# A hybrid decoder layer on one core: own buffers for the raw weights of odd pairs, another order of the early pairs, and low parts moved between VectorE and DMA

## The chip, the cores and the metric

The kernel runs on one core of one Trainium2 chip. The metric is the device time of one execution in microseconds (us). Three runs of the kernel before took 1780.92, 1787.42 and 1790.28 us; the median is 1787.42.

## The reference, cut to what matters

One decoder layer over 1040 positions (16 meta tokens and 1024 inputs) with 1024 channels: a convolution branch and a sparse attention branch are gated, merged and added to the stream, and a gated FFN follows. The change lies in the FFN's up projection:

```python
D_MODEL, D_FF, FFN_CONV_WIDTH = 1024, 2816, 3
...
h = rms_norm(stream, ffn_norm_g[l])
up = causal_depthwise_conv(h @ ffn_up[l], ffn_dw_w[l], ffn_dw_b[l])
a, b_ = jnp.split(up, 2, axis=-1)
stream = stream + (jax.nn.silu(a) * b_) @ ffn_down[l]
```

All data are float32. `h @ ffn_up` multiplies 1024 positions by 1024 x 5632 weights.

## The kernel before, in words

**Products in three parts.** Every float32 operand of a product is split into a high part (a cast to fp32r) and a low part (the operand less its high part). A product is the sum of high x high, high x low and low x high, all in fp32r. A low part is made in one of two ways: by one subtraction on VectorE, or "by DMA", by which ScalarE writes the negated high part into the tile (line 1134 or 1037) and a DMA that accumulates, issued by POOL, adds the raw operand to it (line 1137 or 1038).

**Seven products in place of eight.** The up projection is cut into 22 pairs of 128 output channels (`NPAIR`; one column block of `a` and its partner of `b_`). With the reduction in two halves and the positions in two halves, a pair is a 2 x 2 block product, done with seven products (Strassen's scheme in Winograd's form). The blocks of weights are called A11, A12, A22, N2, S3, S1, S4 (`NAMES`, line 1071). A11, A12 and A22 are pieces of the raw weights; N2, S3, S1 and S4 are sums of pieces, made by four VectorE instructions in place in the two raw tiles `ra` and `rb` of the pair (lines 1121 to 1124). The blocks of rows are B11, B21 and B22 (pieces of the normalized stream `xs2`) and T1 to T4 (sums of pieces: `t12` holds T1 and T2, `t34` holds T3 and T4). `rows_first` makes B11 and B21; `rows_second` (line 1052) makes the others, k tile by k tile (four of them), with high parts `h12`, `h34`, low parts `l12`, `l34`, and both parts of B22 in `B22`.

**Early pairs.** Six pairs (`EARLY`) have their first two products, A11 x B11 and A12 x B21, done ahead (`up_first`), when only the first half of the positions is normalized; their sums wait in tiles `ua`. While TensorE does these twelve products, the second half is normalized and `rows_second` makes the sums. The main loop then does five products for each early pair and seven for each later one. A product is 24 matmuls: four k tiles, two chunks of columns, three parts.

**The order of blocks.** `bseq` (line 1072) lists the blocks of weights in the order of their use. `make_block` (line 1107) makes one: it loads the pair's raw tiles if they are not there (line 1084, on SP's queue), makes the four sums when it comes to N2, casts the high part into the ring tile (line 1132, ScalarE) and makes the low part (line 1134 and 1137, or 1139 on VectorE). The ring has five tiles (`RB`), so blocks are made up to five ahead of their use (`block`, line 1143). The raw tiles share two buffers of tag `wr`: one pair fills them both, and the next pair's loads wait until the last block of this one is made. Blocks A11, A12 and A22 get their low part by DMA, all others on VectorE.

**Tiles and queues.** `ft` gives a tile from 31 buffers, `ft2` one from 7, `tmp` one from 4; a new tile waits until an old one of its kind is read for the last time. A scheduler that works on estimated times puts the instructions of each engine in a fixed order; `urgent()` raises their priority in it. On the chip each engine serves its row in that order and waits by semaphores. SP issues the loads, POOL the accumulating DMAs and the stores of the gated rows (`dB`, `dT`), each in its own row. PSUM has four slots of two banks for these products (`slot`); VectorE's additions (line 1193) free them. After a pair's products, `up_rows` does the convolution of width 3 (line 1219, VectorE), SiLU and the gate.

Of the kernel before, what the change touches and what calls it, by code (L numbers as in the profile page):

```python
# [79 lines left out]
def body(ctx: ExitStack, tc: tile.TileContext, xT, vecs, w_idx, w_v, w_conv, w_k, w_q, w_gate,  # L80
# [970 lines left out]

    def rows_second():

        for k in range(KH):
            b11, b12, b21, b22 = (xs2[o + k][:, c] for o in (0, KH) for c in (c_lo, c_hi))
            t12, t34 = tmp(f"t12_{k}"), ft(f"t34_{k}")
            h12, l12, h34, l34 = (ft(f"{n}_{k}", F32R) for n in ("h12", "l12", "h34", "l34"))
            t = ft(f"B22_{k}", F32R)
            dve.tensor_tensor(t12[:, h0], b12, b11, op=ALU.subtract)
            dve.tensor_tensor(t12[:, h1], b22, t12[:, h0], op=ALU.subtract)  # L1060
            dve.tensor_tensor(t34[:, h1], b21, t12[:, h1], op=ALU.subtract)
            split_block(h34[:, h1], l34[:, h1], t34[:, h1], "T4", k)
            split_block(h12[:, h1], l12[:, h1], t12[:, h1], "T2", k)
            dve.tensor_tensor(t34[:, h0], b22, b12, op=ALU.subtract)
            split_block(h34[:, h0], l34[:, h0], t34[:, h0], "T3", k)
            split_block(h12[:, h0], l12[:, h0], t12[:, h0], "T1", k, True)
            split_block(t[:, h0], t[:, h1], b22, "B22", k, True)


    RB = 5  # L1070
    NAMES = ("A11", "A12", "A22", "N2", "S3", "S1", "S4")
    bseq = [(i, n) for i in range(EARLY) for n in ("A11", "A12")]
    for i in range(NPAIR):
        bseq += [(i, n) for n in NAMES if i >= EARLY or n not in ("A11", "A12")]
    bseq += [(k, "d" + n) for n in NAMES[:-1] for k in range(NG2)]
# [3 lines left out]
    w0, w1 = slice(0, WB), slice(WB, 2 * WB)  # L1079
    raws = {}  # L1080

    def raw_tile(name, src):
        t = base.tile([P, 2 * WB], F32, tag="wr", bufs=2, name=name)
        nc.sync.dma_start(t.rearrange("p (k n) -> p k n", k=src.shape[1]), src)
        return t

# [20 lines left out]
    def make_block():  # L1107
# [3 lines left out]
        if n[0] == "d":  # L1111
            raw = down_raw(i, n[1:])
        else:
            both = i >= EARLY or j >= 2 * EARLY
            if (i, 0) not in raws:
                raws[i, 0] = raw_tile(f"ra{i}", w_up[2 * i])
                if both:
                    raws[i, 1] = raw_tile(f"rb{i}", w_up[2 * i + 1])
            ra, rb = raws[i, 0], raws.get((i, 1))
            if n == "N2":  # L1120
                dve.tensor_tensor(ra[:, w0], ra[:, w0], rb[:, w0], op=ALU.subtract)
                dve.tensor_tensor(rb[:, w0], rb[:, w0], rb[:, w1], op=ALU.add)
                dve.tensor_tensor(rb[:, w1], ra[:, w0], rb[:, w1], op=ALU.subtract)  # L1123
                dve.tensor_tensor(ra[:, w1], ra[:, w1], rb[:, w1], op=ALU.add)
            raw = (ra if n in ("A11", "A12", "S3", "S4") else rb)[:, w0 if n in ("A11", "S3", "S1") else w1]
            if n == "S4":
                del raws[i, 0], raws[i, 1]
            elif n == "A12" and not both:
                del raws[i, 0]
        t = ring[j % RB]  # L1130
        with urgent():
            hi = act.copy(t[:, w0], raw)  # L1132
            if n in ("A11", "A12", "A22"):
                act.activation(t[:, w1], f(t)[:, w0], AF.Copy, scale=-1.0)  # L1134
                a = w_up[2 * i + (n == "A22")]
                kk = slice(0, KH) if n == "A11" else slice(KH, KT)
                pool.dma_start(t[:, w1].rearrange("p (k n) -> p k n", k=KH), a[:, kk], accum_op=ALU.add)  # L1137
            else:
                dve.tensor_tensor(t[:, w1], raw, f(t)[:, w0], op=ALU.subtract)
        if j < RB:  # L1140
# [129 lines left out]
    merge_half(1)  # L1270
    del zh, zl
    norm_half(1)
    for i in range(EARLY):
        early[i] = up_first(i, ft2(f"ua{i}"))
    rows_second()
    xs2.clear()
# [202 lines left out]
```

## Time and profile before

| | |
|---|---|
| median of 3 runs | 1787.42 us (1780.92 to 1790.28) |
| profiled execution | 1788.24 us, span 1786.5 us |
| TensorE busy | 1738.8 us (97% of the span), mean granted clock 0.985 |
| VectorE busy | 1279.8 us (72%) |
| ScalarE busy | 1074.4 us (60%) |
| POOL busy | 282.6 us (16%) |

The span is the time from the first to the last instruction in the profile; the execution's own time lies a little above it. Times in the rows below are in us from the span's start. The merge's last products end at 1086 us, the early products run to 1122.9, the main loop of the up projection to 1553, and the down projection fills the rest. TensorE is busy nearly always, so what matters is where it is not, and at which clock it runs.

### The profile page before, as it was taken

To read this page: it belongs to the slowest core of one execution; us is meant where nothing else is said; L and a number is where in the kernel's file an instruction comes from. 1 tells how busy PE (TensorE), PEld (TensorE's weight loads), DVE (VectorE), ACT (ScalarE), POOL (GpSimd) and SP (SyncE) were. 2 spreads that over 40 slices of the span, in tenths; PEclk is the share of its full clock that TensorE was granted. 3 is DMA by queue.
4 is the path that set the end of the run, shared out by engine and by line. 5 is a ranking of instruction groups with operands and counts; after the bars stand their busy time and mean duration, and the time that the engine had idled before them with its cause. 6 is when DMAs were issued, how large, how long until landed. Compare 5 with 4: busy or idle time off the path is not lost.

```text
span 1786.5 us, 30351 instructions
## 1 busy us (share of the span) xinstructions
PE 1738.8 (97%) x11836; PEld 1676.7 (94%) x11836; DVE 1279.8 (72%) x2107; ACT 1074.4 (60%) x1845; POOL 282.6 (16%) x368
## 2 busy tenths in 40 slices
PE   8999899999999999999999999989999999999997
PEld 8899799999999999899999999889999999988877
DVE  5695598996954493487853465799888888889765
ACT  6766678888998733488842245645455445544561
POOL 1110111111121112122100002212222222110030
PEclk8999999999999999999999999899999999999999
DMA  5653468776656488511246648545544554883372
GB/s 185 143 107 92 107 153 186 168 165 157 159 134 153 125 202 242 142 49 49 79 117 183 207 125 189 113 136 155 155 128 128 150 130 125 284 328 95 94 171 95
DMA packets 93472, 263.72 MB, mean 148 GB/s; under 512 B 10968, under 2 KB 19472, under 8 KB 93328
## 3 DMA queue, kind: packets, MB, share of 16 engines
q0 software_dynamic: 35872, 102.83, 28.3%
q1 hardware_dynamic: 57456, 158.95, 26.9%
q8 instruction: 93, 1.52, 0.3%
q14 instruction: 51, 0.42, 0.1%
HBM read 189.78 MB, written 47.53 MB: 133 GB/s over the span
## 4 chain that ended last, share of the span: by engine, by line
PE 71%; issue 14%; DVE 6%; DMA 5%; ACT 2%; POOL 1%; SPq 0%; POOLq 0%; DVEq 0%; ACTq 0%
PE PS L183 31%; PE PS L1158 21%; PE PS L1002 5%; PE PS L1287 3%; PE PS L914 3%; PE PS L858 3%; PE PS L892 2%; PE PS L460 1%; ACT junk L511 1%; DMA x<-dx 1%; DVE cum L566 1%; DMA rb<-w_up 0%; DMA co<-ct 0%; PE PS L307 0%; DMA ring<-w_up 0%
## 5 line engine op out<-in xcount | busy, mean ns | idle before, releaser
L1158 PE MATMUL PS<-h,ring 128*128 128x256 f32 (+1 forms) x1408 | 191.7, 285 | 11.4 <-DMA ring<-w_up 7.6
L511 ACT ACTIVATE junk<-sc,wn 128x1040 bf16<-128x1040 f32 (+6 forms) x217 | 182.3, 840 | 27.3 <-DVE wn L535 14.4
L183 PE MATMUL PS<-hh,wh 128*128 128x342 f32 (+2 forms) x1096 | 193.4, 327 | 5.2 <-ACT gt L721 1.7
L1158 PE MATMUL PS<-B,ring 128*128 128x256 f32 (+1 forms) x1584 | 195.9, 284 | 0.0
L183 PE MATMUL PS<-hh,wl 128*128 128x342 f32 (+2 forms) x1096 | 192.5, 327 | 3.5 <-DMA wl<-w_conv 3.5
L1158 PEld LDWEIGHTS PS<-B,ring 128*128 128x128 f32 x1584 | 193.6, 192 | 0.0
L1158 PEld LDWEIGHTS PS<-h,ring 128*128 128x128 f32 x1408 | 179.3, 192 | 13.3 <-issue 8.1
L183 PE MATMUL PS<-hl,wh 128*128 128x342 f32 (+2 forms) x1096 | 190.1, 324 | 0.9 <-DMA hl<-x 0.9
L183 PEld LDWEIGHTS PS<-hh,wh 128*128 128x128 f32 x1096 | 179.4, 190 | 9.8 <-ACT gt L721 2.5
L183 PEld LDWEIGHTS PS<-hh,wl 128*128 128x128 f32 x1096 | 180.6, 191 | 5.3 <-DMA wl<-w_conv 3.8
L183 PEld LDWEIGHTS PS<-hl,wh 128*128 128x128 f32 x1096 | 177.3, 188 | 3.3 <-DMA hl<-x 1.7
L127 ACT CAST wh<-wr 128x1024 fp32r<-128x1024 f32 x79 | 82.7, 1046 | 132.9 <-PE PS L183 70.8
L606 DVE SCALAR_TENSOR_TENSOR cb<-g,dwh,cb 128x1026 f32<-128x1026 f32 x105 | 134.4, 1282 | 35.4 <-DMA cb<-ct 35.3
L606 DVE SCALAR_TENSOR_TENSOR co<-g,dwh,co 128x1026 f32<-128x1026 f32 x113 | 144.2, 1281 | 7.6 <-DMA co<-ct 7.5
L1287 PE MATMUL PS<-hlT,ring 128*128 128x512 f32 x528 | 123.1, 394 | 1.1 <-ACT hlT L1242 1.1
L1287 PEld LDWEIGHTS PS<-hlT,ring 128*128 128x128 f32 x528 | 99.0, 188 | 24.6 <-ACT hlT L1242 1.5
L1137 POOL DMA_DIRECT2D ring<-w_up x66 | 58.0, 884 | 327.7 <-ACT ring L1134 207.5
L1132 ACT CAST ring<-ra 128x512 fp32r<-128x512 f32 x88 | 54.2, 617 | 80.8 <-PE PS L1158 62.3
L1158 PE MATMUL PS<-l,ring 128*128 128x258 f32 x704 | 101.7, 287 | 1.1 <-DVE l L1040 1.1
L1132 ACT CAST ring<-rb 128x512 fp32r<-128x512 f32 x66 | 40.9, 620 | 96.2 <-DVE rb L1123 40.4
L1158 PEld LDWEIGHTS PS<-l,ring 128*128 128x128 f32 x704 | 93.0, 194 | 1.4 <-DVE l L1040 1.4
L1193 DVE TENSOR_TENSOR ua<-ua,PS 128x514 f32<-128x514 f32 x66 | 45.2, 685 | 53.0 <-PE PS L1158 53.0
(480 smaller groups left out, 3650.3 us busy)
## 6 DMA issues: line engine op xcount, KB each, us to landing
ring<-w_up POOLq DMA_DIRECT2D x66, 256.0 KB, 4.4
ra<-w_up SPq DMA_DIRECT2D x28, 512.0 KB, 3.6
rb<-w_up SPq DMA_DIRECT2D x22, 512.0 KB, 3.8
dT<-dt POOLq DMA_DIRECT2D x44, 256.0 KB, 4.0
hlT<-dT SPq DMA_DIRECT2D x44, 256.0 KB, 2.7
dB<-us POOLq DMA_DIRECT2D x33, 256.0 KB, 3.8
dth<-gt SPq DMA_DIRECT2D x16, 513.0 KB, 7.7
gate<-dth SPq DMA_DIRECT2D x16, 513.0 KB, 4.7
```

The source lines that it names most:

```text
L127: e = act.copy(wh[:, :nk * P], raw[:, :nk * P])
L183: pe.matmul(ps[:, ci, :n], lhsT=ww[:, sl], rhs=rr[k][:, c0:c0 + n], start=(k == 0 and pi == 0), stop=(k == nk - 1 and pi == 2))
L511: act.activation(junk[:, :n], sc[j][:, PAD:PAD + n], AF.Sign, bias=bits.bitcast(F32)[:, slot[j]:slot[j] + 1], accum_out=cnt[:, slot[j]:slo ...
L606: dve.scalar_tensor_tensor(a, g[:, w:w + LQ], wt[w], a, op0=ALU.mult, op1=ALU.add)
L858: pe.matmul(lg[:, :nn], lhsT=qq[:, qc], rhs=kk[g][:, c0:c0 + nn], start=(pi == 0), stop=(pi == 2))
L914: pe.matmul(ov[:, q0:2 * P], lhsT=vv[g][:, vs], rhs=tt[kb // 4][:, rs_], start=False, stop=(kb == nkb - 1 and pi == 2))
L1002: pe.matmul(ps[:, b, p0:p0 + nn], lhsT=ww[:, k * P:(k + 1) * P], rhs=rr[k][:, c0 + r0:c0 + r0 + nn], start=(k == 0 and pi == 0), stop=(k = ...
L1132: hi = act.copy(t[:, w0], raw)
L1137: pool.dma_start(t[:, w1].rearrange("p (k n) -> p k n", k=KH), a[:, kk], accum_op=ALU.add)
L1158: pe.matmul(ps[:, b, p0:p0 + nn], lhsT=t[:, o + k * P:o + (k + 1) * P], rhs=B[rows][k][e][:, r0:r0 + nn], start=(pi == 0 and k == 0), stop ...
L1193: return dve.tensor_tensor(dst, a, ps, op=op)
L1287: pe.matmul(ps[:, :n], lhsT=w[:, o + m * P:o + (m + 1) * P], rhs=r[:, x * HS + c0:x * HS + c0 + n], start=(k == 0 and pi == 0), stop=(k == ...
```

## The change

Four things are changed, all in the making of the up projection's operands.

1. `raw_tile` takes a source of tiles. In the main loop the raw tiles of odd pairs (all but the last) come from `ft` (pair 1: `ft2`); even pairs keep the two `wr` buffers.
2. The early pairs' first products are done in reverse order, pair 5 first and pair 0 last, and pair 0 loads both its raw tiles then and keeps them for its later blocks.
3. `rows_second` is cut in two loops. The first, with raised priority, makes T1, T2 and T4 and T4's high part for all four k tiles. The second makes all the rest; T1's and B22's low parts are now made on VectorE.
4. The first six blocks get their low parts on VectorE, and S3, S1 and S4 of the six early pairs get theirs by DMA, from the raw tile that holds the sum.

```diff
@@ -1051,25 +1051,35 @@
 
     def rows_second():
 
-        for k in range(KH):
-            b11, b12, b21, b22 = (xs2[o + k][:, c] for o in (0, KH) for c in (c_lo, c_hi))
-            t12, t34 = tmp(f"t12_{k}"), ft(f"t34_{k}")
-            h12, l12, h34, l34 = (ft(f"{n}_{k}", F32R) for n in ("h12", "l12", "h34", "l34"))
+        ks = range(KH)
+        t12, t34, h34 = [], [], []
+        with urgent():
+            for k in ks:
+                b11, b12, b21, b22 = (xs2[o + k][:, c] for o in (0, KH) for c in (c_lo, c_hi))
+                t12.append(tmp(f"t12_{k}"))
+                t34.append(ft(f"t34_{k}"))
+                h34.append(ft(f"h34_{k}", F32R))
+                dve.tensor_tensor(t12[k][:, h0], b12, b11, op=ALU.subtract)
+                dve.tensor_tensor(t12[k][:, h1], b22, t12[k][:, h0], op=ALU.subtract)
+                dve.tensor_tensor(t34[k][:, h1], b21, t12[k][:, h1], op=ALU.subtract)
+                act.copy(h34[k][:, h1], t34[k][:, h1])
+        for k in ks:
+            b12, b22 = xs2[k][:, c_hi], xs2[KH + k][:, c_hi]
+            h12, l12, l34 = (ft(f"{n}_{k}", F32R) for n in ("h12", "l12", "l34"))
             t = ft(f"B22_{k}", F32R)
-            dve.tensor_tensor(t12[:, h0], b12, b11, op=ALU.subtract)
-            dve.tensor_tensor(t12[:, h1], b22, t12[:, h0], op=ALU.subtract)
-            dve.tensor_tensor(t34[:, h1], b21, t12[:, h1], op=ALU.subtract)
-            split_block(h34[:, h1], l34[:, h1], t34[:, h1], "T4", k)
-            split_block(h12[:, h1], l12[:, h1], t12[:, h1], "T2", k)
-            dve.tensor_tensor(t34[:, h0], b22, b12, op=ALU.subtract)
-            split_block(h34[:, h0], l34[:, h0], t34[:, h0], "T3", k)
-            split_block(h12[:, h0], l12[:, h0], t12[:, h0], "T1", k, True)
-            split_block(t[:, h0], t[:, h1], b22, "B22", k, True)
+            dve.tensor_tensor(l34[:, h1], t34[k][:, h1], f(h34[k])[:, h1], op=ALU.subtract)
+            B["T4"][k] = (h34[k][:, h1], l34[:, h1])
+            split_block(h12[:, h1], l12[:, h1], t12[k][:, h1], "T2", k)
+            dve.tensor_tensor(t34[k][:, h0], b22, b12, op=ALU.subtract)
+            split_block(h34[k][:, h0], l34[:, h0], t34[k][:, h0], "T3", k)
+            split_block(h12[:, h0], l12[:, h0], t12[k][:, h0], "T1", k)
+            split_block(t[:, h0], t[:, h1], b22, "B22", k)
+            t12[k] = t34[k] = None
 
 
     RB = 5
     NAMES = ("A11", "A12", "A22", "N2", "S3", "S1", "S4")
-    bseq = [(i, n) for i in range(EARLY) for n in ("A11", "A12")]
+    bseq = [(i, n) for i in reversed(range(EARLY)) for n in ("A11", "A12")]
     for i in range(NPAIR):
         bseq += [(i, n) for n in NAMES if i >= EARLY or n not in ("A11", "A12")]
     bseq += [(k, "d" + n) for n in NAMES[:-1] for k in range(NG2)]
@@ -1079,8 +1089,8 @@
     w0, w1 = slice(0, WB), slice(WB, 2 * WB)
     raws = {}
 
-    def raw_tile(name, src):
-        t = base.tile([P, 2 * WB], F32, tag="wr", bufs=2, name=name)
+    def raw_tile(name, src, spare):
+        t = spare(name)[:, :2 * WB] if spare else base.tile([P, 2 * WB], F32, tag="wr", bufs=2, name=name)
         nc.sync.dma_start(t.rearrange("p (k n) -> p k n", k=src.shape[1]), src)
         return t
 
@@ -1111,11 +1121,12 @@
         if n[0] == "d":
             raw = down_raw(i, n[1:])
         else:
-            both = i >= EARLY or j >= 2 * EARLY
+            both = i >= EARLY or i == 0 or j >= 2 * EARLY
             if (i, 0) not in raws:
-                raws[i, 0] = raw_tile(f"ra{i}", w_up[2 * i])
+                spare = (ft2 if i == 1 else ft) if j >= 2 * EARLY and i % 2 == 1 and i < NPAIR - 1 else None
+                raws[i, 0] = raw_tile(f"ra{i}", w_up[2 * i], spare)
                 if both:
-                    raws[i, 1] = raw_tile(f"rb{i}", w_up[2 * i + 1])
+                    raws[i, 1] = raw_tile(f"rb{i}", w_up[2 * i + 1], spare)
             ra, rb = raws[i, 0], raws.get((i, 1))
             if n == "N2":
                 dve.tensor_tensor(ra[:, w0], ra[:, w0], rb[:, w0], op=ALU.subtract)
@@ -1130,11 +1141,14 @@
         t = ring[j % RB]
         with urgent():
             hi = act.copy(t[:, w0], raw)
-            if n in ("A11", "A12", "A22"):
+            if j >= EARLY and n in ("A11", "A12", "A22"):
                 act.activation(t[:, w1], f(t)[:, w0], AF.Copy, scale=-1.0)
                 a = w_up[2 * i + (n == "A22")]
                 kk = slice(0, KH) if n == "A11" else slice(KH, KT)
                 pool.dma_start(t[:, w1].rearrange("p (k n) -> p k n", k=KH), a[:, kk], accum_op=ALU.add)
+            elif i < EARLY and n in ("S3", "S1", "S4"):
+                act.activation(t[:, w1], f(t)[:, w0], AF.Copy, scale=-1.0)
+                pool.dma_start(t[:, w1], raw, accum_op=ALU.add)
             else:
                 dve.tensor_tensor(t[:, w1], raw, f(t)[:, w0], op=ALU.subtract)
         if j < RB:
@@ -1270,7 +1284,7 @@
     merge_half(1)
     del zh, zl
     norm_half(1)
-    for i in range(EARLY):
+    for i in reversed(range(EARLY)):
         early[i] = up_first(i, ft2(f"ua{i}"))
     rows_second()
     xs2.clear()
```

The change moves instructions on each engine. In the names below the first number is the pair, the k tile or the ring's tile, and the last one is only a tile's running number.

SP's row of loads, where the early part ends and the main loop begins; before (`w_up` is the raw weight):

```order
L1084 DMA ra4_10731<-w_up 128x1024
L1084 DMA ra5_10790<-w_up 128x1024
L1084 DMA ra0_10849<-w_up 128x1024
L1084 DMA rb0_10851<-w_up 128x1024
L1084 DMA ra1_11088<-w_up 128x1024
L1084 DMA rb1_11090<-w_up 128x1024
L1084 DMA ra2_11246<-w_up 128x1024
L1084 DMA rb2_11248<-w_up 128x1024
L1241 DMA hlB11_0_15334<-dB11_9563 128x512
L1084 DMA ra3_11417<-w_up 128x1024
L1084 DMA rb3_11419<-w_up 128x1024
```

and now:

```order
L1094 DMA ra1_10725<-w_up 128x1024
L1094 DMA ra0_10784<-w_up 128x1024
L1094 DMA rb0_10786<-w_up 128x1024
L1094 DMA ra1_11075<-w_up 128x1024
L1094 DMA ra2_11236<-w_up 128x1024
L1094 DMA rb1_11077<-w_up 128x1024
L1094 DMA ra3_11410<-w_up 128x1024
L1094 DMA rb3_11412<-w_up 128x1024
L1094 DMA rb2_11238<-w_up 128x1024
L1094 DMA ra5_11745<-w_up 128x1024
L1094 DMA ra4_11571<-w_up 128x1024
```

The load of `ra0` is there once, `rb0` follows it, and from pair 1 on the loads of odd and even pairs are interleaved: `rb1` stands behind `ra2`, and `ra3`, `rb3` and `ra5` ahead of the rest of their even neighbours.

VectorE's row, where the early products are still running; before (lines 1121 to 1124 are the four sums of a pair's weights):

```order
L1178 TENSOR_TENSOR ua1_10671<-ua1_10671,PS_63 128x514
L1061 TENSOR_TENSOR t34_0_10968<-xr4_9553,t12_0_10967 128x514
L1121 TENSOR_TENSOR ra0_10849<-ra0_10849,rb0_10851 128x512
L1040 TENSOR_TENSOR l34_0_10972<-t34_0_10968,h34_0_10971 128x514
L1122 TENSOR_TENSOR rb0_10851<-rb0_10851 128x512
L1040 TENSOR_TENSOR l34_0_10972<-t34_0_10968,h34_0_10971 128x514
L1040 TENSOR_TENSOR l12_0_10970<-t12_0_10967,h12_0_10969 128x514
L1061 TENSOR_TENSOR t34_1_10991<-xr5_9554,t12_1_10990 128x514
L1064 TENSOR_TENSOR t34_1_10991<-xr5_9554,xr1_9550 128x514
L1178 TENSOR_TENSOR ua3_10789<-ua3_10789,PS_63 128x514
L1123 TENSOR_TENSOR rb0_10851<-ra0_10849,rb0_10851 128x512
```

and now (the four sums are lines 1132 to 1135, T4 is line 1064, T3 line 1073, T4's low part line 1070):

```order
L1192 TENSOR_TENSOR ua4_10665<-ua4_10665,PS_63 128x514
L1064 TENSOR_TENSOR t34_1_10969<-xr5_9554,t12_1_10968 128x514
L1073 TENSOR_TENSOR t34_1_10969<-xr5_9554,xr1_9550 128x514
L1132 TENSOR_TENSOR ra0_10784<-ra0_10784,rb0_10786 128x512
L1064 TENSOR_TENSOR t34_2_10976<-xr6_9555,t12_2_10975 128x514
L1073 TENSOR_TENSOR t34_2_10976<-xr6_9555,xr2_9551 128x514
L1133 TENSOR_TENSOR rb0_10786<-rb0_10786 128x512
L1064 TENSOR_TENSOR t34_3_10983<-xr7_9556,t12_3_10982 128x514
L1073 TENSOR_TENSOR t34_3_10983<-xr7_9556,xr3_9552 128x514
L1070 TENSOR_TENSOR l34_0_10991<-t34_0_10962,h34_0_10963 128x514
L1040 TENSOR_TENSOR l34_0_10991<-t34_0_10962,h34_0_10963 128x514
L1134 TENSOR_TENSOR rb0_10786<-ra0_10784,rb0_10786 128x512
```

All t34 tiles are now made ahead of the first low part, and two of them stand ahead of the first sum of pair 0's weights.

ScalarE's row at the beginning of pair 1's blocks; before:

```order
L1132 CAST ring2_9560<-rb1_11090 128x512
L1134 ACTIVATE ring2_9560<-ring2_9560 128x512
L1132 CAST ring3_9561<-rb1_11090 128x512
L1132 CAST ring4_9562<-ra1_11088 128x512
L1185 COPY ua1_11217<-ua1_10671 128x1028
L1132 CAST ring0_9558<-rb1_11090 128x512
L1132 CAST ring1_9559<-ra1_11088 128x512
```

and now (line 1143 is the cast, line 1145 the negation for A22, line 1150 that for S3, S1 and S4):

```order
L1143 CAST ring2_9560<-rb1_11077 128x512
L1145 ACTIVATE ring2_9560<-ring2_9560 128x512
L1199 COPY ua1_11206<-ua1_10844 128x1028
L1143 CAST ring4_9562<-ra1_11075 128x512
L1143 CAST ring0_9558<-rb1_11077 128x512
L1150 ACTIVATE ring4_9562<-ring4_9562 128x512
L1150 ACTIVATE ring0_9558<-ring0_9558 128x512
L1143 CAST ring3_9561<-rb1_11077 128x512
L1143 CAST ring2_9560<-rb2_11238 128x512
L1143 CAST ring1_9559<-ra1_11075 128x512
L1150 ACTIVATE ring1_9559<-ring1_9559 128x512
```

S3, S1 and S4 have a negation behind their cast now, and pair 2's first cast stands ahead of pair 1's S4. POOL's row has one accumulating DMA for each of these negations, in the same order.

## Rows read from the trace of the kernel before

**Rows 1.** The table of stretches. Columns: from and to (us), length, then for PE (TensorE's matmuls), PEld (its weight loads), DVE (VectorE), ACT (ScalarE) and POOL the busy time in us with the number of instructions, then TensorE's mean granted clock, the share of the DMA engines' time, and GB/s.

```profile
1122.00:1140.00 18.00, 13.99 (x74) 12.48 (x73) 12.28 (x21) 12.85 (x24) 6.10 (x7) 0.72 0.83 163
1140.00:1175.00 35.00, 34.74 (x291) 34.53 (x289) 29.75 (x40) 19.44 (x25) 2.92 (x4) 1.00 0.37 104
1175.00:1221.00 46.00, 37.78 (x284) 37.26 (x285) 40.25 (x57) 18.19 (x25) 8.37 (x14) 0.93 0.45 145
1221.00:1553.00 332.00, 332.00 (x2771) 332.00 (x2770) 276.24 (x371) 167.42 (x236) 74.04 (x105) 1.00 0.55 149
1553.00:1786.00 233.00, 222.50 (x1110) 186.38 (x1108) 169.38 (x293) 104.63 (x190) 23.28 (x36) 0.98 0.53 168
```

**Rows 2.** TensorE in order of time, from the end of the early products on: start, length, engine, line, operation and its tiles, count of merged instructions, and in brackets the idle time before the row and what ended it. `h` and `l` are high and low parts of T1 to T4.

```profile
1122.92 0.64 PE L1158 MATMUL PS<-h,ring 128*128 128x258 f32 x4
...
1130.17 0.80 PE L1158 MATMUL PS<-h,ring 128*128 128x258 f32 x2 [1.57 <-ACT h L1035]
...
1135.07 0.80 PE L1158 MATMUL PS<-l,ring 128*128 128x258 f32 x2 [1.10 <-DVE l L1040]
...
1142.98 2.07 PE L1158 MATMUL PS<-h,ring 128*128 128x258 f32 x16
...
1176.42 1.19 PE L1158 MATMUL PS<-h,ring 128*128 128x258 f32 x8 [1.69 <-DMA ring<-w_up]
...
1193.92 1.74 PE L1158 MATMUL PS<-h,ring 128*128 128x258 f32 x8 [2.89 <-DMA ring<-w_up]
...
1209.01 1.21 PE L1158 MATMUL PS<-h,ring 128*128 128x258 f32 x8 [0.87 <-ACT ring L1132]
...
1214.20 1.57 PE L1158 MATMUL PS<-h,ring 128*128 128x258 f32 x8 [3.04 <-DMA ring<-w_up]
```

**Rows 3.** The table of stretches again (columns as in rows 1), for shorter stretches.

```profile
1130.00:1135.00 5.00, 3.80 (x16) 3.50 (x16) 1.28 (x3) 2.58 (x6) 1.37 (x2) 0.50 1.00 208
1135.00:1140.00 5.00, 4.93 (x24) 4.93 (x25) 3.12 (x6) 2.27 (x5) 2.62 (x3) 0.53 0.75 131
...
1150.00:1175.00 25.00, 24.74 (x207) 24.53 (x205) 24.28 (x32) 16.24 (x20) 2.92 (x4) 1.00 0.40 114
...
1192.00:1200.00 8.00, 6.08 (x38) 6.11 (x39) 4.60 (x7) 1.24 (x2) 0.56 (x1) 0.79 0.32 87
...
1212.00:1221.00 9.00, 6.80 (x44) 6.83 (x45) 7.36 (x13) 1.97 (x4) 1.63 (x3) 0.81 0.67 227
```

**Rows 4.** All engines in order of time, around pair 0's and pair 1's raw tiles (SPq is SP's issue of a load).

```profile
1107.81 0.62 ACT L1132 CAST ring<-ra 128x512 fp32r<-128x512 f32 x1 [0.80 <-PE PS L1158]
1108.46 0.33 SPq L1084 DMA_DIRECT2D rb<-w_up  x1
...
1114.11 0.69 DVE L1121 TENSOR_TENSOR ra<-ra,rb 128x512 f32<-128x512 f32 x1 [3.20 <-ACT B L1035]
...
1127.49 0.33 SPq L1084 DMA_DIRECT2D rb<-w_up  x1
...
1133.72 0.69 DVE L1121 TENSOR_TENSOR ra<-ra,rb 128x512 f32<-128x512 f32 x1 [3.84 <-DMA rb<-w_up]
```

**Rows 5.** From the same view, a run of VectorE instructions and a run of ScalarE casts, each with its total length.

```profile
1107.21 2.50 DVE L1060 TENSOR_TENSOR t<-xr,t 128x514 f32<-128x514 f32 x4
...
1129.51 2.17 ACT L1035 CAST h<-t 128x514 fp32r<-128x514 f32 x4
```

**Rows 6.** The instructions on the ring's tiles, over the whole span: count, shortest, median and longest time in ns, first and last start, shapes.

```profile
L1134 ACT ACTIVATE ring<-ring x66: 612/633/638, 1075.4 to 1527.8; 128x512 fp32r<-128x512 f32 x66
L1137 POOL DMA_DIRECT2D ring<-w_up x66: 850/871/1221, 1076.3 to 1529.1; - x66
L1132 ACT CAST ring<-rb x66: 602/621/626, 1116.1 to 1532.5; 128x512 fp32r<-128x512 f32 x66
L1139 DVE TENSOR_TENSOR ring<-rb,ring x44: 679/683/693, 1123.8 to 1533.9; 128x512 fp32r<-128x512 f32 x44
```

**Rows 7.** The page's list of DMA issues: queue, count, size of each, median us from issue to landing; over the whole span.

```profile
ring<-w_up POOLq DMA_DIRECT2D x66, 256.0 KB, 4.4
ra<-w_up SPq DMA_DIRECT2D x28, 512.0 KB, 3.6
rb<-w_up SPq DMA_DIRECT2D x22, 512.0 KB, 3.8
```

**Rows 8.** Line 1038, the accumulating DMAs of T1's and B22's low parts, whose raw operand lies in SBUF: POOL's time to issue them in ns, and their us from issue to landing.

```profile
L1038 POOL DMA_DIRECT2D l<-t x4: 862/862/867, 1117.8 to 1135.5; - x4
L1038 POOL DMA_DIRECT2D B<-xr x4: 862/1172/1242, 1118.3 to 1136.1; - x4
...
DMA to landing us min/median/max: 3.3/4.8/6.8
```

**Rows 9.** From the view of the tiles `rb`, 1100 to 1235 us: us from issue to landing of seven loads.

```profile
DMA to landing us min/median/max: 3.2/3.4/4.7
```

**Rows 10.** Line 1137, POOL's issues of accumulating DMAs from 1150 to 1175 us, in ns.

```profile
L1137 POOL DMA_DIRECT2D ring<-w_up x2: 871/884/896, 1155.9 to 1172.3; - x2
```

**Rows 11.** VectorE's groups of instructions from 1150 to 1175 us: line, operation, tiles, shapes, count, busy us, mean ns, idle us before them and its releaser.

```profile
L1219 DVE SCALAR_TENSOR_TENSOR us<-ua,vec,us 128x1024 f32<-128x1024 f32 x4 | 5.1, 1280 | 0.7 <-ACT us L1217 0.7
...
L1221 DVE TENSOR_TENSOR us<-us,ut 128x1024 f32<-128x1024 f32 x2 | 2.4, 1218 | 0.0
```

## The prediction

> **What bounds the kernel now.** I read the table of stretches first [rows 1], then TensorE's instructions in order of time [rows 2], then the stretches with a low clock [rows 3], then what the late instructions waited for [rows 4]. From 1221 to 1553 us TensorE is busy all the time and shows 2771 matmuls in 332.0 us, 0.120 us each [rows 1]; this is its own rate in the up projection, and nothing there can be won by moving other engines' work. From 1122 to 1221 us it shows 74, 291 and 284, together 649 matmuls [rows 1]; at 0.120 us they need 77.9 us and take 99. So 21.1 us are lost between the start of pair 0's second part and pair 5, and nearly nowhere else: after 1553 us the down projection runs on what this change leaves alone.
>
> The loss has two parts. From 1122 to 1140 us, 74 matmuls worth 8.9 us take 18: 9.1 us lost. TensorE reaches pair 0's sum products at 1122.9, stops for the casts and low parts of T4 to T1 (1.57 and 1.10 us are the longest stops), and starts pair 1's first product, eight matmuls into the row at 1142.98, at 1143.9 [rows 2]. In the stops the granted clock falls to 0.50 and 0.53, the 1.2 GHz level [rows 3]. The cause stands on VectorE: its N2 sum of pair 0 waits from 1110.9 to 1114.1 and that of pair 1 3.84 us to 1133.7, each for a raw tile issued 5.7 and 6.2 us before [rows 4] (the first wait is put down to a cast, but the sum reads the two raw tiles alone, and only the load was still out), with all splits queued behind. From 1175 to 1221 us, 284 matmuls worth 34.1 us take 46: 11.9 us lost. The stops of 1.69, 2.89 and 3.04 us wait for the low part of an A22 block, the one of 0.87 us for a cast [rows 2]; each is the tail of one chain: last use of the two raw buffers, two loads, cast, negation, accumulating DMA. After two of them the clock is 0.79 and 0.81 over 8 and 9 us [rows 3].
>
> **The change, part by part.** Count first. In the six early pairs S3, S1 and S4 lose 18 low parts on VectorE, and gain 18 negations on ScalarE and 18 accumulating DMAs on POOL; the first six blocks go the other way (6 low parts to VectorE, 6 negations and 6 DMAs gone), and so do T1 and B22 (8). Net: VectorE -4, ScalarE +4, POOL +4, SP -1 load. What matters is where.
>
> *First six blocks on VectorE* (0.68 us each [rows 6]): cost 0. They lie under the merge products, where TensorE is busy and VectorE waits for it; if that cover failed, TensorE would wait about 0.7 us per block, 4 us at most.
>
> *Reverse order, rb of pair 0 early, first sums ahead.* Pair 0's rb still goes into the buffer that the cast of the A11 block in the third ring leaves at about 1108.4 (before: cast at 1107.81, issue at 1108.46 [rows 4]), so it lands at about 1113.8 as before. But VectorE now does two t34 tiles ahead of that wait and has 32 instructions left from the N2 sum on, among them eight more low parts. Four such instructions take 2.50 us, 0.60 apart [rows 5]: 1113.8 + 32 x 0.60 = 1133.0. ScalarE, four casts in 2.17 us or 0.54 apart [rows 5], ends its splits near 1130. TensorE wants them one after another from 1122.9 on and the last at 1133. Walking both rows side by side I find one stop of 0.7 us (the T2 cast of the last k tile); bounds 0 and 4.0, the idle time of now (18.0 less 14.0 busy [rows 1]). TensorE would be through pair 0's interleaved products at 1122.9 + 96 x 0.120 + 0.7 = 1135.1.
>
> *Pair 1's own room.* Its ra is free to load at once, but its rb stands in SP's row behind pair 2's ra, which needs the buffer of pair 0's rb, and that is now read by an accumulating DMA (S1's low part). S1's negation stands 22 places behind the cast that the first sum lets go at 1114.5 on ScalarE, 0.54 each: about 1126.5. The DMA from one tile in SBUF to another took 3.3, 4.8 and 6.8 us (least, median, most) [rows 8]; 1131.3 with the median. SP issues ra of pair 2, then rb of pair 1 at 1131.7. A load lands in 3.4 us (median of this stretch [rows 9]), 5.7 to 6.2 in the busy spots [rows 4]; five loads now stand one behind the other, so I take 5.0: 1136.7. With the cast of 0.62 [rows 6], TensorE starts pair 1 at 1137.4: a stop of 2.3 us; bounds 0 (3.3 and 3.4 us) and 5.3 (6.8 and 6.2). A stop of 1.69 us left the clock alone, one of 2.89 cost 1.5 us (38 matmuls in 6.1 us instead of 4.6 [rows 2, 3]); I take half, 0.8. Before, this point was reached at 1143.9: 1143.9 - 1137.4 - 0.8 = 5.7 us won.
>
> *Pairs 2 to 5.* An early pair is five products, 120 matmuls, 14.4 us. VectorE's share of it was 16 short instructions of 0.60 (6 adds, 4 sums, 4 low parts, 2 differences on average) and five long ones of 1.2 (1.28 and 1.22 with an overlap of 0.08 [rows 5, 11]): 15.6 us, more than TensorE's, and it was busy for 24.28 of 25 us from 1150 to 1175 [rows 3]. Without three low parts it is 13.8 us. ScalarE's share rises by three negations of 0.63 [rows 6] to some 10 us and POOL's by three issues of 0.87, so both stay below 14.4. Odd pairs' raw tiles stand a whole pair ahead, so A22's chain (cast 0.62, negation 0.63, DMA 4.4 [rows 6, 7]) has 8 us or more where it had none: the 11.9 us go. What is late next: VectorE's sums for pairs 4 and 5 stand early in its row, while these pairs' rb waits for the accumulating DMA of pair 2's S4 and pair 3's S1. By the same durations VectorE stops 2 to 5 us there, with about that much lead over TensorE's four PSUM slots. I put 2.2 us of new stops; bounds 0 and 6.
>
> The Trainium skill (DMA: Bandwidth & Descriptors, Anatomy of one DMA) gives a transfer issued from GpSimd 2.0 us plus its bytes at 436 GB/s; that would be 2.6 us for 256 KB, an estimate by that page. No accumulating DMA here landed under 3.3 us, and the medians are 4.4 and 4.8 [rows 7, 8]. By the page pair 1's stop and its clock would go and the time be 3.1 us shorter, 1770; I keep the rows.
>
> Sum: 5.7 + 11.9 - 2.2 = 15.4 us won. The profiled execution took 1788.2 us (span 1786.5 and 1.7 around it), so 1772.8, say 1773; the median shown is 0.8 lower than that execution, which lies inside the spread of the three runs.
>
> **Rivals.** *All stops go.* Pair 1's rb lands in time and VectorE keeps its lead; only 0.7 is left of 21.1: 1788.2 - 20.4 = 1767.8. For it: raw tiles a pair ahead, and 1.8 us a pair freed on VectorE. Against: two accumulating DMAs now stand in the way of a load.
>
> *Most is given back inside the early pairs.* The added DMAs meet the burst of loads: pair 1 stops for 5.3 + 1.5, and pairs 4 and 5 for 3 us each with 1.5 of clock once; with the 0.7 it is 15.0, so 6.1 us won: 1782. For it: in 1130 to 1135 us the DMA engines were already full (share 1.00) and loads took 6.2 us [rows 3, 4]. Against: the share is 0.40 from 1150 to 1175. The Trainium skill (SBUF - State Buffer, Who interferes with whom) says that VectorE in a two-port mode and GpSimd block each other for a whole instruction; by it each of POOL's new issues could wait for one of VectorE's, and this rival would be likelier. With VectorE busy 24.28 of 25 us, POOL's issues took 0.88 us [rows 10] against 0.87 over all [rows 6], so I give it no more for that.
>
> *Slower: the loads form one line.* SP's row is served in order, and behind each even pair's load, held until an accumulating DMA has landed, stands an odd pair's. If the landings stay at their longest (6.8 and 6.2 us), every pair from 1 to 5 starts 5.3 us late with 1.5 of clock: 5 x 6.8 + 0.7 = 34.7 against 21.1, 13.6 lost: 1802. It decides from 4.2 us a pair (21.1 / 5). Against: from pair 3 on a load has a whole pair of time, 14.4 us.
>
> **How the numbers follow.** Forecast 1773 with 0.57 (its own range 1768 to 1779), all stops gone 0.14, most given back 0.22, slower 0.07. About 0.5%, 8.9 us, is what a measurement of this kernel can tell from no change: bounds 1778.5 and 1796.3. Faster: 0.53 of the first, 0.14, and a quarter of the third, 0.72; same: 0.04 and 0.17, 0.21; slower 0.07. The range goes from 1766 to 1783.
>
> **What would show it.** Right: no stop for a T block over 1 us and the clock 1.00 up to 1135; a stop of 1 to 4 us at pair 1's A22, released by rb's landing; 120 matmuls per 14.4 us afterwards; VectorE busy some 0.96 there. Wrong: DMA waits at pairs 2 to 5 as now, or VectorE named as releaser of most stops; new stops at 1553 us, where the down projection's rows are now loaded later, since the odd raw tiles hold their buffers.

## The result and the profile after

The changed kernel took 1770.4 us, the median of 4 runs (1765.77 to 1771.79), beside 1786.88 us of 4 runs of the kernel before (1780.92 to 1790.28): ratio 0.9904, 95% interval 0.9882 to 0.9925. It is faster by more than the 0.5% that counts here. The profiled execution took 1771.79 us with a span of 1770.0; before it was 1788.24 with 1786.5. All times in this document leave out two executions of 5.82 ms, one each of the runs "S3, S1, S4 low on VectorE" and "before + reverse and T rows".

The table of stretches of the kernel after, columns as in rows 1, answers to [rows 1]:

```profile
1122.00:1140.00 18.00, 16.77 (x141) 16.56 (x140) 14.41 (x25) 11.27 (x21) 2.63 (x4) 1.00 0.67 191
1140.00:1175.00 35.00, 35.00 (x294) 35.00 (x293) 31.32 (x42) 25.20 (x36) 12.36 (x16) 1.00 0.69 152
1175.00:1221.00 46.00, 44.73 (x373) 44.55 (x372) 40.91 (x54) 27.49 (x39) 15.22 (x21) 1.00 0.79 217
1221.00:1553.00 332.00, 330.84 (x2698) 327.61 (x2697) 276.87 (x374) 170.14 (x239) 71.41 (x103) 1.00 0.55 155
```

141 matmuls stand where 74 stood, and 373 where 284 stood; the clock is 1.00 in all four rows. The DMA engines work more (0.69 and 0.79 where they showed 0.37 and 0.45); VectorE is 40.91 us busy in the third row, as before (40.25), for a third more matmuls. The last row no longer holds the up projection alone. The first three rows also show what the 21.1 us lost before were: TensorE was idle for 12.5 us (99 less 86.5 busy [rows 1]), and the other 8.6 were matmuls slower than 0.120 us, 7.0 of them in the stretches with a low clock [rows 3]. Now 2.5 us are idle and 808 matmuls take 96.5 us, 0.119 each: more than a third of the gain is the clock that stays up when the stops go.

TensorE in order of time, columns as in rows 2, every stop (idle time in brackets) from pair 0's second part to the down projection (the first row is pair 0's first T product, the last one the down projection's first product):

```profile
1125.09 1.11 PE L1172 MATMUL PS<-h,ring 128*128 128x258 f32 x8
...
1137.96 1.23 PE L1172 MATMUL PS<-h,ring 128*128 128x258 f32 x8 [1.24 <-ACT ring L1143]
...
1179.83 1.20 PE L1172 MATMUL PS<-h,ring 128*128 128x258 f32 x8 [1.27 <-ACT ring L1143]
...
1538.31 61.67 PE L1301 MATMUL PS<-hlB,ring 128*128 128x512 f32 x264 [1.16 <-DVE ua L1207]
```

Of the six stops in [rows 2] two short ones are left, at pair 1 and pair 4. One measure serves for all that follows: the us from TensorE's first up product to its first down product, read from two rows of a trace. Before it is 1554.15 - 1086.17 = 468.0, after 1538.31 - 1088.31 = 450.0: 18.0 won. The measure is taken from one execution of each kernel. The first up product came 2.1 us later than before; over the traces of this study it lies anywhere from 1082.6 to 1088.5, so that is scatter of what comes ahead. What follows the first down product is 0.7 us shorter: 2.1 - 18.0 - 0.7 = -16.6, the spans' difference but for rounding.

All engines in order of time around pair 0's and pair 1's raw tiles, as in [rows 4]:

```profile
1110.34 0.33 SPq L1094 DMA_DIRECT2D rb<-w_up  x1
...
1113.63 0.69 DVE L1132 TENSOR_TENSOR ra<-ra,rb 128x512 f32<-128x512 f32 x1 [0.45 <-DMA rb<-w_up]
...
1127.34 0.86 POOL L1151 DMA_DIRECT2D ring<-rb  x1 [5.30 <-ACT ring L1150]
...
1130.84 0.33 SPq L1094 DMA_DIRECT2D ra<-w_up  x1
1131.26 0.87 SPq L1094 DMA_DIRECT2D rb<-w_up  x1
...
1137.29 0.62 ACT L1143 CAST ring<-rb 128x512 fp32r<-128x512 f32 x1 [6.70 <-DMA rb<-w_up]
```

The first two rows are pair 0's rb: issued at 1110.34, summed 3.3 us later, where it was 5.65 before [rows 4]. The last four are the chain forecast for pair 1: S1's accumulating DMA, ra of pair 2 released by it, rb of pair 1 behind, its cast 6.0 us after the issue.

### The profile page after: what moved, and what is told of

It reads as the page before. It is cut to its first block, busy times and chain, and to the rows that moved or that the text cites. A ratio compares the mean times of both kernels' runs of the same rounds, so it can differ in the third digit from the quotient of the medians.

```text
span 1770.0 us, 30414 instructions
## 1 busy us (share of the span) xinstructions
PE 1731.8 (98%) x11836; PEld 1671.5 (94%) x11836; DVE 1276.6 (72%) x2103; ACT 1078.3 (61%) x1849; POOL 285.4 (16%) x372
## 3 DMA queue, kind: packets, MB, share of 16 engines
q8 instruction: 93, 1.52, 0.3%
## 4 chain that ended last, share of the span: by engine, by line
PE 71%; issue 14%; DMA 6%; DVE 5%; ACT 2%; POOL 2%; SPq 0%; POOLq 0%; DVEq 0%; ACTq 0%
PE PS L183 31%; PE PS L1172 22%; PE PS L1002 5%; PE PS L914 3%; PE PS L858 3%; PE PS L1301 2%; PE PS L892 2%; PE PS L460 1%; ACT junk L511 1%; DMA rb<-w_up 1%; DMA hlB<-dB 1%; DMA x<-dx 1%; DVE cum L566 1%; DMA wl<-w_conv 0%; DMA co<-ct 0%
## 5 line engine op out<-in xcount | busy, mean ns | idle before, releaser
L511 ACT ACTIVATE junk<-sc,wn 128x1040 bf16<-128x1040 f32 (+6 forms) x217 | 182.3, 840 | 19.5 <-DVE wn L535 10.1
L1172 PE MATMUL PS<-B,ring 128*128 128x258 f32 (+1 forms) x1584 | 193.9, 282 | 0.0
L1172 PE MATMUL PS<-h,ring 128*128 128x258 f32 (+1 forms) x1408 | 188.1, 283 | 2.5 <-ACT ring L1143 2.5
L1148 POOL DMA_DIRECT2D ring<-w_up x60 | 52.6, 877 | 297.6 <-ACT ring L1145 158.2
L134 ACT ACTIVATE wl<-wr 128x1024 fp32r<-128x1024 f32 x60 | 63.3, 1055 | 36.3 <-PE PS L183 36.1
```

The costliest lines, as they stand in the source:

```text
L134: act.activation(wl[:, :nk * P], raw[:, :nk * P], AF.Copy, scale=-1.0)
L511: act.activation(junk[:, :n], sc[j][:, PAD:PAD + n], AF.Sign, bias=bits.bitcast(F32)[:, slot[j]:slot[j] + 1], accum_out=cnt[:, slot[j]:slo ...
L1172: pe.matmul(ps[:, b, p0:p0 + nn], lhsT=t[:, o + k * P:o + (k + 1) * P], rhs=B[rows][k][e][:, r0:r0 + nn], start=(pi == 0 and k == 0), stop ...
```

## The experiments

Each run was timed against the kernel before on its chip; "stretch" is the measure above, "low by DMA" and "low on VectorE" say how low parts are made.

| run | stretch, us | time, us | ratio to before (95%) |
|---|---|---|---|
| before / after | 468.0 / 450.0 | 1786.9 / 1770.4 | 0.9904 (0.9882 to 0.9925) |
| after, no own rooms | 466.0 | 1788.4 | 0.9991 (0.9978 to 1.0004) |
| after, S3, S1, S4 low on VectorE | 455.0 | 1771.2 | 0.9897 (0.9866 to 0.9927) |
| after, forward order | 455.0 | 1776.0 | 0.9923 (0.9902 to 0.9945) |
| after, T rows as before | 461.2 | 1784.5 | 0.9968 (0.9953 to 0.9982) |
| after, T1 and B22 low by DMA | 458.9 | 1780.4 | 0.9945 (0.9925 to 0.9966) |
| after, first six low by DMA | 457.3 | 1778.4 | 0.9946 (0.9928 to 0.9963) |
| before + rooms | 461.6 | 1783.9 | 0.9963 (0.9943 to 0.9984) |
| before + reverse and T rows | 465.3 | 1785.4 | 0.9981 (0.9959 to 1.0003) |
| before + S3, S1, S4 low by DMA | 475.7 | 1796.2 | 1.0035 (1.0014 to 1.0056) |
| after, rb of pair 1 first | 449.8 | 1769.6 | 0.9890 (0.9871 to 0.9910) |
| after, six DMAs doubled | 457.5 | 1777.8 | 0.9938 (0.9920 to 0.9956) |

**No own rooms.**

```diff
-                spare = (ft2 if i == 1 else ft) if j >= 2 * EARLY and ...
+                spare = None
```

> The kernel after, with odd pairs' raw tiles back in the two shared buffers; everything else kept. My theory (the rooms are what removes the 11.9 us lost at pairs 2 to 5, and the low parts by DMA need them, since such a DMA holds a raw buffer some 5 us longer than VectorE's subtraction did): every early pair from 1 to 5 waits for S1's DMA, a load, a cast, a negation and a DMA; stops of 3 to 6 us at each A22, several of them with a low clock behind; 1785 to 1800 us, slower than before or about like it. Rival (what was short before was VectorE's time, and the 18 low parts taken off it are the gain; the rooms are an extra): 1770 to 1775 us, no stop over 1.5 us.

16.0 us of the 18.0 are gone. TensorE's stops in order of time:

```profile
1135.89 1.23 PE L1172 MATMUL PS<-h,ring 128*128 128x258 f32 x8 [0.93 <-ACT ring L1143]
...
1170.43 1.66 PE L1172 MATMUL PS<-h,ring 128*128 128x258 f32 x8 [4.64 <-ACT ring L1143]
...
1209.88 2.08 PE L1172 MATMUL PS<-h,ring 128*128 128x258 f32 x8 [6.38 <-ACT ring L1143]
```

These are A22 of pairs 1, 3 and 5, waiting for the cast that waits for rb; pairs 2 and 4 wait 0.54 and 1.52 us for A22's low part. The theory holds with its size; only its 3 to 6 us at "every pair" was too wide.

**S3's, S1's and S4's low parts back on VectorE** (the three lines under `elif i < EARLY` go).

> The kernel after, with S3's, S1's and S4's low parts of the early pairs back on VectorE. My theory (VectorE needs 15.6 us a pair of 14.4 us without the DMAs): pair 1 starts without its 1.2 us stop, since ra2 no longer waits for a DMA, but the T blocks come 1 to 2 us later and pairs 2 to 5 lose about 1 us each, with VectorE as the releaser; 1773 to 1778 us. Rival (the rooms alone are enough, VectorE catches up in the lead of the PSUM slots): 1766 to 1771 us, at most one stop of 1 us.

The time, 1771.2 us, lies between my range and the rival's, and its ratio to before, 0.9897, is not told from the 0.9904 of the kernel after; the 5.0 us are seen in the stretch of one execution alone. VectorE was the releaser of 0.45 us of stops in the early pairs and of 1.59 at the last pair, not of one a pair; and pair 1's stop grew to 4.10 us instead of going. It is A22's own accumulating DMA, issued at 1130.48, in the middle of the loads that are now let go sooner. POOL's issue, TensorE's stop, and the table of two stretches (columns as in rows 1):

```profile
1130.48 0.86 POOL L1148 DMA_DIRECT2D ring<-w_up  x1 [12.22 <-ACT ring L1145]
...
1136.98 2.05 PE L1169 MATMUL PS<-h,ring 128*128 128x258 f32 x8 [4.10 <-DMA ring<-w_up]
```

```profile
1130.00:1135.00 5.00, 2.88 (x25) 2.67 (x23) 2.34 (x5) 2.08 (x4) 0.86 (x1) 1.00 0.95 317
1135.00:1140.00 5.00, 3.02 (x14) 3.05 (x15) 5.00 (x10) 1.56 (x4) 0.00 (x0) 0.67 0.05 9
```

It landed after 6.4 us, with the DMA engines 0.95 busy, and the clock then stood at 0.67.

**Forward order** (`reversed` and `or i == 0` taken out).

> The kernel after, with the early pairs in the order 0 to 5 again and rb of pair 0 loaded where it was. My theory (rb of pair 0 landed at 1113.6 us here and at 1114.1 us before, so the reversal moved nothing that TensorE waits for): within 2 us of the kernel after, 1768 to 1773 us. Rival (the reversal is what brings the first sums, and with them the T blocks, in time): first sum waits 3 us as before, stops at the T blocks of 3 to 6 us, 1774 to 1780 us.

My theory fell: 5.0 us of the stretch are lost (the ratios' intervals, 0.9902 to 0.9945 and 0.9882 to 0.9925, overlap). All engines in order of time:

```profile
1105.53 0.33 SPq L1094 DMA_DIRECT2D rb<-w_up  x1
...
1111.60 0.69 DVE L1132 TENSOR_TENSOR ra<-ra,rb 128x512 f32<-128x512 f32 x1 [3.23 <-issue]
...
1130.49 0.87 POOL L1148 DMA_DIRECT2D ring<-w_up  x1 [2.36 <-DVE ra L1132]
...
1139.13 3.77 PE L1172 MATMUL PS<-h,ring 128*128 128x258 f32 x16 [3.93 <-DMA ring<-w_up]
```

Without `i == 0` ra of pair 0 is loaded a second time, 2.6 us ahead of rb; the first sum came 6.1 us after rb's issue, and A22's DMA of pair 1, issued at 1130.49, let TensorE go on only at 1139.13, after a stop of 3.93 us. The rival had the late sum and the time right, but not the place of the stop, which is no T block. The order and the second load were taken together here, so which of the two costs the 5.0 us is not shown.

**T rows as before** (`rows_second` of the kernel before).

> The kernel after, with the T blocks made tile by tile as before (sums of a k tile right ahead of its low parts, T1's and B22's low parts by DMA). My theory (the order of VectorE's row, t34 ahead of the wait for rb, and the DMAs kept out of T1 and B22 remove the 9.1 us lost between 1122 and 1140 us): stops at the T blocks of 3 to 8 us in all with a clock near 0.5 to 0.8 behind them; 1775 to 1780 us. Rival (the T blocks were late because VectorE waited for the load alone): stops under 2 us, 1769 to 1773 us.

11.2 us lost: stops of 1.78, 0.52, 0.47 and 2.27 us at T blocks and 3.52 behind VectorE at pair 1. TensorE's two longest:

```profile
1140.67 0.51 PE L1162 MATMUL PS<-l,ring 128*128 128x258 f32 x2 [2.27 <-DMA l<-t]
...
1145.65 2.05 PE L1162 MATMUL PS<-h,ring 128*128 128x258 f32 x8 [3.52 <-DVE ua L1197]
```

The theory holds, with more than it gave. Which of its two halves does it, the next run shows.

**T1 and B22 low by DMA, in the new row** (`True` put back in the two `split_block` calls).

> The kernel after, with T1's and B22's low parts by DMA as before, in the new order of the row. My theory (in the run with the old T rows it is the order, the low parts queued ahead of the wait for rb, that cost most of 11.2 us; the DMAs the smaller part): 450 to 453 us, stops under 2 us. Rival (the eight DMAs are the cause: they meet the loads): a stop of 2 to 4 us with <-DMA l or B, 454 to 461 us.

8.9 us lost, so the eight DMAs alone cost most of the 11.2, and the old order, beside them, adds 2.3: the rival. But the stop is not at a T block. All engines in order of time, and then the landing times of the eight DMAs, from the view of their line:

```profile
1127.30 0.96 POOL L1151 DMA_DIRECT2D ring<-rb  x1
...
1133.22 0.71 SPq L1094 DMA_DIRECT2D rb<-w_up  x1
...
1142.24 0.62 ACT L1143 CAST ring<-rb 128x512 fp32r<-128x512 f32 x1 [9.06 <-DMA rb<-w_up]
...
1142.91 2.08 PE L1172 MATMUL PS<-h,ring 128*128 128x258 f32 x8 [9.24 <-ACT ring L1143]
```

```profile
DMA to landing us min/median/max: 3.3/5.5/12.6
```

It is the chain of pair 1 again: S1's DMA lets the load of ra of pair 2 go 5.5 us after its issue instead of 3.5, then rb takes 9.0 us instead of 6.0, beside up to eight DMAs of T1 and B22.

**First six blocks' low parts by DMA** (`j >= EARLY and` taken out), which the prediction costed at nothing.

> The kernel after, with the first six blocks' low parts by DMA as before. My theory (these blocks lie under the merge products, where nobody waits for them, and their DMAs are over long before the burst of loads): 450 to 451 us of the same stretch, no new stop, 1768 to 1773 us in all. Rival (their DMAs run into the loads of the first raw tiles, as T1's and B22's did later): a stop of 1 us or more among the early products, 452 to 456 us.

7.3 us lost; the rival, with its stop among the early products (1.21 us), and more. Pair 0's rb in order of time; then the accumulating DMAs issued from 1090 to 1120 us (count, size, median us to landing), of this run and of the kernel after:

```profile
1110.15 0.33 SPq L1094 DMA_DIRECT2D rb<-w_up  x1
...
1117.10 0.69 DVE L1132 TENSOR_TENSOR ra<-ra,rb 128x512 f32<-128x512 f32 x1 [4.50 <-DMA rb<-w_up]
```

```profile
ring<-w_up POOLq DMA_DIRECT2D x8, 256.0 KB, 6.3
```

```profile
ring<-w_up POOLq DMA_DIRECT2D x6, 256.0 KB, 3.7
```

The six DMAs put back are issued 17.8 us or more ahead of this load and are not themselves in its way, but the early products' later blocks now come at other times: POOL issues one of their DMAs at 1109.00, 1.15 us ahead of rb's load, where the kernel after has none for the 4.2 us ahead of it. rb takes 6.95 us to its sum instead of 3.3. Over the traces without doubled DMAs it splits the same way: 3.3 to 3.9 us in the six kernels with the first blocks on VectorE and pair 0's ra kept, 5.3 to 7.0 in the five with them by DMA, before among these; forward order, with its second load of ra, took 6.1.

**Six DMAs doubled** in the kernel after, to test that by itself:

```diff
                 pool.dma_start(t[:, w1]..., a[:, kk], accum_op=ALU.add)
+                if j < 2 * EARLY:
+                    pool.dma_start(t[:, w1]..., a[:, kk], accum_op=ALU.add)
```

> The kernel after, with six accumulating DMAs doubled: the low parts of the early A blocks seven to twelve are added twice (these low parts are then raw twice less the high part, so only the time is read). No other instruction is added, SP's row is the same, and VectorE's is the same up to the first sums. My theory (a raw tile's load that has such DMAs in flight beside it lands in 5 to 7 us instead of 3.3, and this is what delayed pair 0's sums in before and in the run with the first blocks by DMA): rb of pair 0 is summed 4.5 to 7 us after its issue instead of 3.3, VectorE waits 2 to 4 us there, 452 to 458 us from the first up to the first down product. Rival (the rows' order is the cause, not the DMAs): 3.3 to 3.6 us, 450 to 451 us.

All engines in order of time, and TensorE's first stop:

```profile
1108.96 0.33 SPq L1094 DMA_DIRECT2D rb<-w_up  x1
...
1115.72 0.69 DVE L1132 TENSOR_TENSOR ra<-ra,rb 128x512 f32<-128x512 f32 x1 [3.92 <-DMA rb<-w_up]
...
1118.38 13.31 PE L1174 MATMUL PS<-B,ring 128*128 128x258 f32 x88 [5.07 <-DMA ring<-w_up]
```

With the DMAs alone added, rb takes 6.8 us and VectorE waits 3.92: the theory. The stretch says nothing of what the late sum costs, since a doubled DMA runs behind its first and holds an early block itself: the 5.07 us, with a clock of 0.62 from 1118 to 1126, bring TensorE to the T blocks 7.8 us later, and from there on the stretch is as short as in the kernel after (412.9 and 413.2).

**One part alone, on the kernel before.** Own rooms:

> The kernel before, with own rooms for odd pairs' raw tiles and nothing else. Measure: us from TensorE's first up product to its first down product, 468.0 before, 450.0 after. My theory (the two losses are separate; the rooms remove the 11.9 us of pairs 2 to 5, less the 2.2 us of stops behind VectorE that the run with the low parts on VectorE showed): 458 us (456 to 461), 1777 to 1781 us in all, the T blocks' stops as before. Rival (early loads meet the accumulating DMAs of T1, B22 and A22, as in the two runs where a DMA landed 6 to 9 us after its issue): T stops longer than before or A22 of pair 1 late by 4 us, 463 to 468 us.

6.4 us won, between the two. From the first T product on the stretch is 10.0 us shorter, as the theory had it; ahead of it TensorE came 3.6 us later, since the first loads now go out beside the DMAs of the first blocks (rb 6.35 us). Reverse order and T rows, run a second time for the profile (1786.9 us, one execution):

> The kernel before, with the early pairs in reverse, rb of pair 0 early and the T blocks' new row, nothing else. My theory (separate losses): the T stops go, those at A22 of pairs 3 to 5 stay: 459 us (457 to 462). Rival (the raw tiles set a period of their own, some 17 us a pair, so that whoever comes 9 us earlier waits 9 us more at pairs 2 to 5): 464 to 468 us, with A22 stops of 3 to 5 us from pair 1 on.

> The kernel of the run with the rows alone, once more for its profile: its time was 0.9981 of before, 3.4 us won where the T blocks' stops had cost 9.1. My theory now (the shared raw buffers set a period of their own, so that TensorE waits at A22 what it saved at the T blocks): T stops under 1 us, A22 stops of 2 to 5 us from pair 1 or 2 on, 9 to 13 us in all, 463 to 466 us of the same stretch. Rival (the T stops stay, since VectorE's row has other waits there): T stops of 4 us and more, A22 stops as before.

Only 2.7 us won: the rival of the first text, the theory of the second. TensorE's stops at A22 of pairs 1 to 5:

```profile
1142.17 1.18 PE L1168 MATMUL PS<-h,ring 128*128 128x258 f32 x8 [0.59 <-DMA ring<-w_up]
1158.33 1.20 PE L1168 MATMUL PS<-h,ring 128*128 128x258 f32 x8 [1.53 <-DMA ring<-w_up]
1174.34 1.19 PE L1168 MATMUL PS<-h,ring 128*128 128x258 f32 x8 [1.36 <-DMA ring<-w_up]
...
1192.89 1.74 PE L1168 MATMUL PS<-h,ring 128*128 128x258 f32 x8 [2.95 <-DMA ring<-w_up]
...
1213.60 1.93 PE L1168 MATMUL PS<-h,ring 128*128 128x258 f32 x8 [3.20 <-DMA ring<-w_up]
```

They add up to 9.6 us where they were 7.6 [rows 2], 11.5 with two waits for a cast where it was 8.5, with 1.7 left at the T blocks: part of what is saved ahead of pair 1 is waited for at the shared buffers. Low parts by DMA:

> The kernel before, with the early pairs' S3, S1 and S4 low parts by DMA and nothing else. My theory (such a DMA holds the shared raw buffer about 5 us longer than VectorE's low part, and with no own room every pair's load waits for it): A22 stops of 3 to 6 us at most early pairs; 478 to 490 us, 1797 to 1810 us in all. Rival (VectorE's time was what was short before, and this frees it): 460 to 466 us.

7.7 us lost, a little less than forecast; the theory, though its stops from pair 1 on are 0.5 to 2.9 us and not 3 to 6. The loads are waited for longer: from 1100 to 1240 us VectorE's first sums wait 14.6 us for rb and 3.8 more put down to "issue", 18.4 in all, where it was 7.0 before, the two waits of [rows 4].

**rb of pair 1 in the room that is free first**, ra in the other.

> The kernel after, with pair 1's rb in the room that is free at 1110 us and its ra in the other; the two change places in SP's row, everything else kept. Measure: us from TensorE's first up product to its first down product, 450.0 after. My theory (the 1.24 us stop at pair 1 is rb of pair 1, issued only when S1's DMA has landed and the early tile of pair 0 has been copied): rb lands 15 us earlier, the stop goes, and the N2 sum now waits for ra instead, which TensorE wants one product later, so little or nothing comes back: 448.5 to 449.5 us. Rival (the N2 chain of pair 1 is as late: ra lands at the same time, sums, cast and low part follow): a stop of 1 to 3 us moves to N2, 450 to 452 us.

The stop at A22 went and one came at the next step, the rival: TensorE waits 1.71 us for a PSUM slot that VectorE frees late, because its N2 sum waits 1.5 us for ra.

```profile
1139.74 3.12 PE L1171 MATMUL PS<-B,ring 128*128 128x258 f32 x24 [1.71 <-DVE ub L1206]
```

Of 18.0 us, single parts taken out lose 16.0, 5.0, 5.0, 8.9 and 7.3 of the stretch, together far more, and alone on the kernel before they win 6.4 and 2.7 or lose 7.7. They don't add: each opens the way for the next. The two losses of 5.0 are the weakest of these, since the times do not tell those kernels from the kernel after.

## Why the prediction was right, and where it was not

*The loss before.* Right: 18.0 of the 21.1 us went from the stretch named, and no more than 0.7 from behind it.

*Pair 0 and pair 1.* Forecast 5.7 us won, measured 8.1: from the first up product to pair 1's first product 1143.9 - 1086.17 = 57.7 before and 1137.96 - 1088.31 = 49.65 after. The chain was the one described, with S1's DMA, ra of pair 2 and rb of pair 1 in this order; the load took 6.0 us (5.0 was put), the DMA 3.5 (4.8), the stop 1.24 (2.3), and the clock stayed (0.8 was put). T2's stop of 0.7 did not come. The Trainium skill (DMA: Bandwidth & Descriptors, Anatomy of one DMA) would give 2.6 us for this DMA, an estimate by that page; the trace shows 0.9 more.

*"First six blocks on VectorE: cost 0" and "it lands at about 1113.8 as before"* are the step that failed. rb took 3.3 us instead of 5.65 to its sum, and VectorE's 32 instructions ended 7.9 us after TensorE reached the T blocks (1133.03 - 1125.09), not 10.1 (1133.0 - 1122.9). That the sum stands at 1113.63 and the last instruction ends at 1133.03, as forecast, is luck: rb was issued 1.9 us later than put, like all ahead of it, and its load was some 2 us shorter. Put back, this edit costs 7.3 us. The prediction looked for what the edit costs VectorE, and not for what it takes out of POOL's queue. The same holds for T1 and B22: it counted "eight more low parts" on VectorE and gave nothing for eight DMAs less, which are worth 8.9. The sum came out well all the same, because the prediction put nearly all of the 9.1 us down to VectorE's new order, which brings them only together with these two edits.

*Pairs 2 to 5.* Forecast 11.9 - 2.2 = 9.7; from pair 1's first product to the first down product it is 410.25 us before and 400.35 after, 9.9 won. One new stop of 1.27 us came, at pair 4: VectorE waited 3.48 us for the next pair's rb ahead of pair 4's third sum, and N2's cast for VectorE. It is the mechanism named, at one of the two pairs named:

```profile
1177.78 0.69 DVE L1132 TENSOR_TENSOR ra<-ra,rb 128x512 f32<-128x512 f32 x1 [3.48 <-DMA rb<-w_up]
...
1179.17 0.62 ACT L1143 CAST ring<-rb 128x512 fp32r<-128x512 f32 x1 [4.25 <-DVE rb L1134]
```

The rooms carry it, as the first run shows. VectorE was 0.89 busy (40.91 of 46 us) and not 0.96: its share of a pair was put too high, and the run with the low parts back on it lost only 0.45 us behind it in the early pairs.

*The rivals.* "All stops go" (1767.8) is nearer than "most is given back" (1782), and the measured median lies between it and the forecast. The loads did not form one line in the kernel after; with one part missing they did (the stops of 9.24, 4.64 and 6.38 us in the experiments). The down projection's start lost 0.6 us, the new stops feared at 1553.

## What to carry to other kernels

Moving work off a DMA queue had a gain of its own here (7.3 and 8.9 us), because a load was waited for nearby: look at which transfers are in flight when the load on the path is issued, and not only at the engine that takes the work over. Parts that share one chain (buffers, loads, low parts) have to be judged together: low parts by DMA lost 7.7 us alone and did no harm, and in one trace saved 5.0, beside the others. The last stop of about a microsecond moved to the next operand when it was taken away, from rb to ra of pair 1. And count the clock with the stops: of the 21.1 us lost, 8.6 were not idle time but slow matmuls.

## What the runs showed of the hardware

The same 512 KB load (pair 0's rb, from its issue to the sum that waits for it) took 3.3 to 3.9 us with no accumulating DMA issued in the 4 us ahead of it, and 5.3 to 7.0 with one issued some 1.2 us ahead. In forward order, with none in the 4 us ahead but with ra loaded 2.6 us ahead, it took 6.1. Pair 1's rb took 9.0 beside the DMAs of T1 and B22. An accumulating DMA of 256 KB, 3.6 us in the median of the kernel after's line 1151, took 6.4 and 8.5 us in a burst of loads (the runs with low parts back on VectorE and with forward order), with the DMA engines' share at 0.93 to 1.05.
